# Average pooling over one axis: sixteen tile loads dealt out to two DMA queues

## The chip, the core and the metric

The kernel runs on one core of one Trainium2 chip. The time is device microseconds (us) from the start to the end of one execution; a median of several runs is quoted, and a profile comes from one execution of its own. Five engines of the core can issue instructions: TensorE (PE, not used here), VectorE (DVE), ScalarE (ACT), GpSimd (POOL) and SyncE (SP). Transfers between the chip's memory (HBM) and the on-chip buffers (SBUF) are done by 16 DMA engines. An instruction on SP's or on ACT's queue starts a transfer; it then runs by itself and raises a semaphore when it has landed.

## The reference

The input is 32 x 256 rows of 4096 float32 values. Each row is cut into 256 windows of 16 values, and the output is the mean of each window.

```python
batch, channels, length = 32, 256, 4096
output_size = 256
result = np.zeros((batch, channels, output_size), dtype=np.float32)
for i in range(output_size):
    start = int(i * length / output_size)
    end = int((i + 1) * length / output_size)
    result[:, :, i] = np.mean(x[:, :, start:end], axis=-1)
```

134.22 MB are read, 8.39 MB are written, and each input value takes part in one addition.

## The kernel before

The 8192 rows are put on 128 partitions and cut into 16 tiles. A tile has four rows in each partition (`R = 4`), which are 16,384 float32 values or 64 KB in one piece; a whole tile is 8.39 MB. It has 1024 windows (`cells`) in each partition, and `m = 512` is half of them.

The loop runs over `t` from 0 to 15. For each tile:

- **Load (L64).** One DMA on SP's queue fills the buffer `xin`. The pool `inpool` has two buffers, so tile t+2 goes into the buffer of tile t: its load waits until the last instruction that reads tile t is done. SP's queue holds all the loads, in order, and the loads of tiles 0 and 1 wait for nothing.
- **POOL (L68)** adds, in the second half of the windows, the upper eight values onto the lower eight, in place.
- **DVE (L73)** sums the first half of the windows, 16 values each. It needs nothing from POOL.
- **DVE (L76)** sums the second half of the windows, of which eight values each are left. It needs POOL's result, and it is the last reader of `xin`.
- **ACT (L79)** multiplies the tile's 1024 sums by 1/16, in place in the result tile. It reads no `xin`.

Results stay on the chip until the end: tile 0's in `res_first` and the others' in `res_rest`. In the last turn of the loop three stores are issued on SP's queue: tile 0's result (L66, 512 KB) and the results of tiles 1 to 14 (L67, 7168 KB), both after the last load in the queue, and tile 15's result (L85, 512 KB) at the end.

The program is written with a tile framework that puts in the semaphore waits. It also settles where each instruction stands in the queue of its engine; an engine takes the instructions of its queue in that order. In SP's queue before, they stand as in the source: 16 loads, then the three stores.

Of the kernel before, what the change touches and what calls it, by code (L numbers as in the profile page):

```python
# [1 line left out]

# [4 lines left out]


@with_exitstack
def kernel(  # L10
    ctx: ExitStack,
    tc: tile.TileContext,
    x: bass.AP,
    output_size: int,
    out: bass.AP,
):

    nc = tc.nc
    F32 = mybir.dt.float32
    X = mybir.AxisListType.X

    batch, channels, length = x.shape
    ob, oc, olen = out.shape
    assert ob == batch and oc == channels and olen == output_size
    assert length % output_size == 0
    window = length // output_size  # L30
    hw = window // 2
    inv_w = 1.0 / float(window)

    P = nc.NUM_PARTITIONS
    R = 4
    rows = batch * channels
    assert rows % (P * R) == 0
    ntiles = rows // (P * R)
    many = (ntiles - 1) * R
    cells = R * output_size  # L40
    m = cells // 2
    cols = R * length

    xr = x.rearrange("b c l -> (b c) l")
    orow = out.rearrange("b c o -> (b c) o")
    x_first = xr[0 : P * R, :].rearrange("(p r) l -> p (r l)", p=P, r=R)
    o_first = orow[0 : P * R, :].rearrange("(p r) o -> p (r o)", p=P, r=R)
    x_rest = xr[P * R :, :].rearrange("(p r) l -> p (r l)", p=P, r=many)
    o_rest = orow[P * R :, :].rearrange("(p r) o -> p (r o)", p=P, r=many)

    inpool = ctx.enter_context(tc.tile_pool(name="inpool", bufs=2))
    respool = ctx.enter_context(tc.tile_pool(name="respool", bufs=1))
    res_first = respool.tile([P, cells], F32, name="res_first")
    res_rest = respool.tile([P, (ntiles - 1) * cells], F32, name="res_rest")
    held = (ntiles - 2) * cells

    for t in range(ntiles):
        xin = inpool.tile([P, cells, window], F32, name="xin")
        if t == 0:
            res, base, src = res_first, 0, x_first  # L60
        else:
            res, base = res_rest, (t - 1) * cells
            src = x_rest[:, (t - 1) * cols : t * cols]
        nc.sync.dma_start(out=xin.rearrange("p o w -> p (o w)"), in_=src)  # L64
        if t == ntiles - 1:
            nc.sync.dma_start(out=o_first, in_=res_first[:, :])  # L66
            nc.sync.dma_start(out=o_rest[:, 0:held], in_=res_rest[:, 0:held])  # L67
        nc.gpsimd.tensor_add(  # L68
            out=xin[:, m:cells, 0:hw],
            in0=xin[:, m:cells, 0:hw],  # L70
            in1=xin[:, m:cells, hw:window],
        )
        nc.vector.reduce_sum(  # L73
            out=res[:, base : base + m], in_=xin[:, 0:m, :], axis=X
        )
        nc.vector.reduce_sum(  # L76
            out=res[:, base + m : base + cells], in_=xin[:, m:cells, 0:hw], axis=X
        )
        nc.scalar.mul(  # L79
            out=res[:, base : base + cells],  # L80
            in_=res[:, base : base + cells],
            mul=inv_w,
        )
        if t == ntiles - 1:
            nc.sync.dma_start(out=o_rest[:, base:], in_=res[:, base:])  # L85


# [1 line left out]
_INS = ['x', 'output_size']  # L89
_OUTS = [((32, 256, 256), 'float32')]  # L90

_NUMBERS = {'output_size': 256}


# [26 lines left out]
```

## Time and profile before

| What | Time |
|---|---|
| Median of 3 runs | 335.19 us (335.05 to 335.36) |
| The profiled execution, its own time | 334.91 us |
| Its span, first to last instruction in the trace | 333.1 us |
| DVE busy | 209.7 us (63%), 32 reductions |
| POOL busy | 139.7 us (42%), 16 additions |
| ACT busy | 18.2 us (5%), 16 multiplications |
| Transfers | 142.61 MB, 428 GB/s over the span |

The share of an engine is its busy time over the span. A row of the page that starts with a line number (L68) names a group of like instructions, how many there were, the mean duration of one in ns, and the time in which the engine stood idle before them, with what ended it. In the timeline the columns are the start in us, the duration in us, the engine, and the instruction; "SPq" is the queue of SP, and a row there is the issue of a transfer and not the transfer itself.

### The profile page before, as it was taken

The numbers are of one execution on the slowest core, as the hardware profiler recorded it, in microseconds if no ns is written. First come the engines' busy times: TensorE is split into PE (matmuls) and PEld (weight loads), VectorE is DVE, ScalarE is ACT, GpSimd is POOL, SyncE is SP. The second block draws the span as 40 slices with busy tenths as digits, with TensorE's granted clock in tenths as the row PEclk, the third lists the DMA queues.
The fourth block names the chain that finished last, engine by engine and source line by source line (L and its number), as shares of the span: only waits on it lengthen the run. The fifth ranks groups of instructions, "written<-read, shape, count | busy, mean of one in ns | idle before, by whom it ended". The sixth has DMA issues, their size and how long they took to land.

```text
span 333.1 us, 159 instructions
## 1 busy us (share of the span) xinstructions
DVE 209.7 (63%) x32; ACT 18.2 (5%) x17; POOL 139.7 (42%) x20
## 2 busy tenths in 40 slices
DVE  0029396693929569392957839295784929578491
ACT  1000101000010100001010100101010010101001
POOL 0027090643709063370906336090733609073460
DMA  9898989999898989999898989989898989989996
GB/s 378 378 504 378 504 378 464 417 393 488 378 504 378 504 378 472 409 401 480 378 504 378 504 378 464 417 386 496 378 504 378 504 378 464 417 386 496 409 441 283
DMA packets 2736, 142.61 MB, mean 428 GB/s; under 512 B 304, under 2 KB 304, under 8 KB 560
## 3 DMA queue, kind: packets, MB, share of 16 engines
q1 hardware_dynamic: 2736, 142.61, 99.1%
HBM read 134.22 MB, written 8.39 MB: 428 GB/s over the span
## 4 chain that ended last, share of the span: by engine, by line
DMA 66%; POOL 18%; DVE 11%; POOLq 3%; issue 0%; ACT 0%; SPq 0%
DMA xin<-in_x_dram 66%; POOL xin L68 18%; DVE res_rest L76 11%; POOLq L116 3%; ACT res_rest L79 0%; SPq L64 0%; POOLq L68 0%
## 5 line engine op out<-in xcount | busy, mean ns | idle before, releaser
L68 POOL TENSOR_TENSOR xin<-xin 128x4096 f32<-128x4096 f32 x16 | 139.5, 8717 | 181.8 <-DMA xin<-in_x_dram 181.8
L73 DVE TENSOR_REDUCE res_rest<-xin 128x512 f32<-128x8192 f32 x15 | 130.3, 8686 | 91.2 <-DMA xin<-in_x_dram 91.2
L76 DVE TENSOR_REDUCE res_rest<-xin 128x512 f32<-128x4096 f32 x15 | 66.3, 4420 | 2.6 <-POOL xin L68 2.4
L79 ACT ACTIVATE res_rest<-res_rest 128x1024 f32<-128x1024 f32 x15 | 15.8, 1056 | 274.5 <-DVE res_rest L76 274.5
L73 DVE TENSOR_REDUCE res_first<-xin 128x512 f32<-128x8192 f32 x1 | 8.7, 8686 | 22.6 <-DMA xin<-in_x_dram 22.6
L76 DVE TENSOR_REDUCE res_first<-xin 128x512 f32<-128x4096 f32 x1 | 4.4, 4419 | 0.1
L79 ACT ACTIVATE res_first<-res_first 128x1024 f32<-128x1024 f32 x1 | 1.1, 1056 | 33.8 <-DVE res_first L76 33.8
L79 ACT ACT_TABLE_LOAD x1 | 1.3, 1283 | 0.7 <-PEq L102 0.7
L102 POOL MEMSET const-float32-0.0<- 128x1 f32 x1 | 0.1, 98 | 0.2 <-issue 0.2
L102 POOL MEMSET const-bfloat16-1.0<- 128x1 bf16 x1 | 0.1, 101 | 0.0
L102 POOL MEMSET const-uint8-127<- 128x1 uint8 x1 | 0.1, 101 | 0.0
L102 POOL MEMSET const-float32-1.0<- 128x1 f32 x1 | 0.1, 98 | 0.0
## 6 DMA issues: line engine op xcount, KB each, us to landing
out_dram<-res_rest SPq DMA_DIRECT2D x1, 7168.0 KB, 23.1
out_dram<-res_first SPq DMA_DIRECT2D x1, 512.0 KB, 26.2
out_dram<-res_rest SPq DMA_DIRECT2D x1, 512.0 KB, 4.9
xin<-in_x_dram SPq DMA_DIRECT2D x16, 25.4
```

Source lines behind the costliest of these rows:

```text
L68: nc.gpsimd.tensor_add(out=xin[:, m:cells, 0:hw], in0=xin[:, m:cells, 0:hw], in1=xin[:, m:cells, hw:window],)
L73: nc.vector.reduce_sum(out=res[:, base : base + m], in_=xin[:, 0:m, :], axis=X)
L76: nc.vector.reduce_sum(out=res[:, base + m : base + cells], in_=xin[:, m:cells, 0:hw], axis=X)
L79: nc.scalar.mul(out=res[:, base : base + cells], in_=res[:, base : base + cells], mul=inv_w,)
L102: nc = _bacc.Bacc("TRN2", target_bir_lowering=False, num_devices=1)
L116: with _tile.TileContext(nc) as tc:
```

## The change

The loads of tiles 1, 3, 5 and so on stay on SP's queue; those of tiles 2, 4, 6 and so on go to ACT's queue. The load of tile 0 is cut by columns into two transfers of 32 KB for each partition, one on each queue. Of the stores, tile 0's and tile 15's go to ACT's queue; the large one stays on SP's.

```diff
-        nc.sync.dma_start(out=xin.rearrange("p o w -> p (o w)"), in_=src)
+        xin_2d = xin.rearrange("p o w -> p (o w)")
+        if t == 0:
+            half = cols // 2
+            nc.sync.dma_start(out=xin_2d[:, 0:half], in_=src[:, 0:half])
+            nc.scalar.dma_start(out=xin_2d[:, half:], in_=src[:, half:])
+        else:
+            queue = nc.sync if t % 2 else nc.scalar
+            queue.dma_start(out=xin_2d, in_=src)
         if t == ntiles - 1:
-            nc.sync.dma_start(out=o_first, in_=res_first[:, :])
+            nc.scalar.dma_start(out=o_first, in_=res_first[:, :])
             nc.sync.dma_start(out=o_rest[:, 0:held], in_=res_rest[:, 0:held])
...
         if t == ntiles - 1:
-            nc.sync.dma_start(out=o_rest[:, base:], in_=res[:, base:])
+            nc.scalar.dma_start(out=o_rest[:, base:], in_=res[:, base:])
```

In the built program, ACT's queue then stands as follows (`mul` is the multiplication of a tile):

```
load 0 (second half), table load, mul 0, load 2, mul 1, store of tile 0, mul 2,
load 4, mul 3, mul 4, load 6, mul 5, mul 6, load 8, ... load 14,
mul 13, mul 14, mul 15, store of tile 15
```

SP's queue holds the first half of load 0, the loads 1, 3, 5 to 15, and the large store. On ACT the load of tile t+2 carries no wait on DVE of its own, since it stands behind `mul t`, which waits for L76 of tile t.

## The prediction

> **What bounds the kernel now.** I read the transfers first, then the chain that ended last, then one period in the timeline, then the tail. The transfers, from the page (row by slice in tenths, packets, queue with its share of the 16 engines' span):
>
> ```profile
> DMA  9898989999898989999898989989898989989996
> DMA packets 2736, 142.61 MB, mean 428 GB/s; under 512 B 304, under 2 KB 304, under 8 KB 560
> q1 hardware_dynamic: 2736, 142.61, 99.1%
> ```
>
> The DMA engines work 99.1% of the span, so no wait on a compute engine costs time yet. Packets: 2736 less 560 small ones is 2176, which is 16 loads x 128 partitions = 2048 of 64 KB and 128 of the large store. A load is thus 8 packets on each of 16 engines.
>
> The chain that ended last, in order of time, its start and one period of it (start, duration, what):
>
> ```profile
> 0.73 0.37 SPq L64
> 1.10 0.05 issue
> 1.15 40.74 DMA xin<-in_x_dram
> ...
> 274.16 0.09 issue
> 274.25 8.73 POOL xin L68
> 282.98 0.02 issue
> 283.01 4.43 DVE res_rest L76
> 287.44 0.02 issue
> 287.45 25.37 DMA xin<-in_x_dram
> ```
>
> This looks as if compute were on the path. The timeline of the same stretch, and of the end, says why it is not:
>
> ```profile
> 22.60 8.69 DVE L73 TENSOR_REDUCE res_first<-xin 128x512 f32<-128x8192 f32 x1 [22.60 <-DMA xin<-in_x_dram]
> ...
> 274.14 8.69 DVE L73 TENSOR_REDUCE res_rest<-xin 128x512 f32<-128x8192 f32 x1 [6.08 <-DMA xin<-in_x_dram]
> 287.45 0.33 SPq L64 DMA_DIRECT2D xin<-in_x_dram  x1
> 287.46 1.06 ACT L79 ACTIVATE res_rest<-res_rest 128x1024 f32<-128x1024 f32 x1 [18.30 <-DVE res_rest L76]
> 293.49 8.69 DVE L73 TENSOR_REDUCE res_rest<-xin 128x512 f32<-128x8192 f32 x1 [6.06 <-DMA xin<-in_x_dram]
> 307.88 0.34 SPq L67 DMA_DIRECT2D out_dram<-res_rest  x1
> 312.84 8.69 DVE L73 TENSOR_REDUCE res_rest<-xin 128x512 f32<-128x8192 f32 x1 [6.08 <-DMA xin<-in_x_dram]
> 327.24 0.33 SPq L85 DMA_DIRECT2D out_dram<-res_rest  x1
> ```
>
> Tile 13 lands at 274.14, tile 14 at 293.49, tile 15 at 312.84: a load takes L = 19.35 us (433 GB/s; 2.42 us a packet). From tile 13's landing to the issue of load 15 it is 13.31 us. So load 15 is issued while load 14 still has 293.49 - 287.45 = 6.04 us to go, and queues behind it. These 6.04 us are all the slack that two buffers leave. The span is: tile 0 lands at 22.60, 15 x 19.35 = 290.24 to 312.84, then 8.39 MB of stores, of which the last is issued at 327.24 and lands 4.9 later (the page's DMA issues), 1.0 to the end: 333.1. With 1.8 around it the profiled run is 334.91; the median is 0.28 above.
>
> **The change, part by part.**
>
> *Nothing to win on volume.* The same 142.61 MB pass the same engines. Idle are at most 0.9% of 333.1 = 3.0 us, nearly all at start and end. The halved first load brings the two halves at one time: 8.39 MB either way, 0 us; 128 more packets and one more issue (0.33 us) lie under the wait for the data. ACT's table load (1.28 us) moves behind that issue and has until 35.85: 0.
>
> *Ten issues on ACT.* Seven whole loads, a half and two stores: 10 x 0.33 to 0.42 = 3.3 to 4.2 us on an engine that stands idle 274.5 us before its multiplications: 0 in busy time. Behind a waiting load on ACT stands `mul t+1`, which is due 19 us later and whose result only a store wants: 0. If that cover went, each would cost its 0.3 us.
>
> *A later issue.* Before, SP issued 0.02 us after L76. Now the even loads stand behind `mul t`: x = 1.06 us if the queue holds the issue until the multiplication is over, 0.02 if it does not, 1.39 if the issue takes its 0.33 after it as well. No row shows it. I take 1.06. By itself it lies inside the 6.04.
>
> *Tile 0's store* moves from behind load 15 to the time of load 3: 512 KB at 433 GB/s = 1.2 us, less at the end, more in the middle: 0. Tile 15's store follows its multiplication either way (327.24), and the large store, which ends later, hides it: 0. The large store still waits for `mul 14`, behind load 15 in SP's queue.
>
> *Two loads in flight on two queues: the step that decides.* Before, load t+2 could only follow load t+1. Now it stands in another queue, and nothing in the program makes it wait. No row of before has two queues, so the bounds are: the older load is served first (lands as now, price 0), or both get half, and a load with r us left lands r late. How much is left? A transfer takes some time from issue to its first byte: at least 0.42 us (the chain has the first DMA from 1.15, issue 0.73), at most 21.87 - 19.35 = 2.52 (first load, 0.73 to 22.60). So of the 6.04 the two overlap for S = 3.5 to 5.6; I take the middle, 4.6, since the first load's 2.52 also holds the start from an empty memory.
>
> With halves: load t+1 lands r late, so its compute and the issue of load t+3 are r late, while load t+2 has got r ahead. The next overlap is S - r, and less x if the next is issued on ACT. From ACT load to ACT load the overlap thus falls by x: the j-th sees S - jx. With 4.6 and 1.06 these are 3.5, 2.5, 1.4, 0.4, then -0.7, -1.8, -2.8, and the eighth in this chain, the large store behind `mul 14`, -3.9. A negative number is a time in which both queues are empty: nothing is left to move until the multiplication of the late tile is over. The sum is 0.7 + 1.8 + 2.8 + 3.9 = 9.2 us, and 335.19 + 9.2 = 344.4. Bounds: S = 5.6 gives 0.8 + 1.8 + 2.9 = 5.5 (340.7); S = 3.5 gives 14.3 (349.5); x = 0.02 gives no drift and 0 us; x = 1.39 with S = 4.6 gives 18.7 (353.9).
>
> If the queues take turns by whole packets instead, the overlap is rounded: 4.6 us is two packets left and a delay of 2.42, which leaves 4.6 - 2.42 - 1.06 = 1.1 us for the next ACT load: no gap, 0 us. But with three packets left (over 4.84 us, which the 1.2 us of tile 0's store beside load 3 can bring about) the delay is 4.84, and each ACT load from tile 6 on, and the large store, meets a gap of 4.84 + 1.06 - 4.6 = 1.3 us: 6 x 1.3 = 7.8 (343.0).
>
> The row for sharing is the 99.1% above: full engines have no rate to give a second queue. [...]
>
> **The rivals.**
>
> *Older load first (or turns that stay balanced): no change.* Place: the 6.04 us before each landing. It decides if the load ahead is delayed by no more than S - x = 3.5 us at each ACT load. For it: before shows strict order in one queue, and the balanced case above. Against: nothing orders two queues. Time: 335.2, with 0.1 to 0.3 either way for packets and start: 334.9 to 335.6.
>
> *Faster: store beside load.* Tile 0's store reads the buffers that loads write; on two queues the two directions might pass at once. That saves at most its 1.2 us, and perhaps a few tenths of the first load's 2.5 us start: 335.19 - 1.2 = 334.0. Against: the stores of before run at the loads' pace (8.39 MB between 312.84 and 332.1, 436 GB/s), so an engine is the limit either way.
>
> *Much slower: convoy.* If a load ahead is delayed until both land together, the queues stay empty for two tiles' compute, 2 x 13.3 less their overlap, in each pair: tens of us, over 353. For it: x of 1.39 or an S of 3.5 brings the gaps to 5 to 8 us by the end. Against: the built order has load t+2 ahead of `mul t+1`, so ACT never holds it for the other tile.
>
> **How the numbers follow.** Sharing with gaps 0.54 (344.4; its own range 340.5 to 351), older first or balanced 0.33 (335.2), store beside load 0.08 (334.0), convoy 0.05. A difference under 0.2% (0.67 us) is no change here, which is about what runs of this kernel can tell. So faster 0.08, same 0.33, slower 0.59. The range takes in the no-change case and the sharing case up to 351: 334.9 to 351.
>
> **What would show it.** In the profile after: two queues, 2880 packets (128 for the halves, 16 for one more transfer). Right: landings (starts of the first DVE reduction) at uneven distances, one near 14 to 15 us and the next near 24 to 26, zeros or low digits in the DMA row that grow towards the end, even loads issued 1.1 us after their L83. Wrong: landings 19.35 us apart throughout, or alternating about 17 and 22 with the DMA share still at 99%; an even load issued beside its multiplication (x near 0); the odd loads' time to landing not above the 25.4 of before.

## The result, and the profile after

The kernel after takes 343.56 us (median of 5 runs, 343.26 to 344.0) beside 335.05 us before (5 runs, 334.99 to 335.36): a ratio of 1.0253, 95% interval 1.0241 to 1.0264. It is 2.5% slower. The profiled span grew from 333.1 to 342.2 us, by 9.1.

The page of the kernel after, the same rows as before:

```profile
DMA  8999998998989899999899999998999998999796
DMA packets 2880, 142.61 MB, mean 417 GB/s; under 512 B 320, under 2 KB 320, under 8 KB 576
q1 hardware_dynamic: 1440, 78.64, 53.4%
q10 hardware_dynamic: 1440, 63.96, 44.2%
```

SP's queue is q1, ACT's is q10. Together they fill 97.6% of 342.2 us, which is 334.0; before it was 99.1% of 333.1, which is 330.1. The bytes are the same. So of the 9.1 us, 5.2 are time in which DMA engines had nothing to do (8.2 against 3.0), and 3.9 are packets that took longer.

The chain of waits of the kernel after, in order of time, one period (start, duration, what):

```profile
161.06 8.73 POOL xin L75
169.79 0.02 issue
169.81 4.43 DVE res_rest L83
174.24 0.02 issue
174.26 26.71 DMA xin<-in_x_dram
```

The links are those of before; the compute took no longer (8.73 and 4.43). The transfer's link was 25.37 and is 26.71. The timeline of the kernel after, around two of ACT's loads (start, duration, engine; SPq and ACTq are issues):

```profile
117.57 0.33 ACTq L71 DMA_DIRECT2D xin<-in_x_dram  x1
121.13 8.69 DVE L80 TENSOR_REDUCE res_rest<-xin 128x512 f32<-128x8192 f32 x1 [3.65 <-DMA xin<-in_x_dram]
...
134.44 0.33 SPq L71 DMA_DIRECT2D xin<-in_x_dram  x1
...
146.44 8.69 DVE L80 TENSOR_REDUCE res_rest<-xin 128x512 f32<-128x8192 f32 x1 [12.03 <-DMA xin<-in_x_dram]
...
159.75 1.06 ACT L86 ACTIVATE res_rest<-res_rest 128x1024 f32<-128x1024 f32 x1 [24.26 <-DVE res_rest L83]
159.84 0.33 ACTq L71 DMA_DIRECT2D xin<-in_x_dram  x1
160.95 8.69 DVE L80 TENSOR_REDUCE res_rest<-xin 128x512 f32<-128x8192 f32 x1 [1.23 <-DMA xin<-in_x_dram]
...
186.50 8.69 DVE L80 TENSOR_REDUCE res_rest<-xin 128x512 f32<-128x8192 f32 x1 [12.27 <-DMA xin<-in_x_dram]
...
200.99 8.69 DVE L80 TENSOR_REDUCE res_rest<-xin 128x512 f32<-128x8192 f32 x1 [1.21 <-DMA xin<-in_x_dram]
```

Landings are read from the starts of a tile's first reduction. Tiles 5 to 9 land at 121.13, 146.44, 160.95, 186.50 and 200.99: distances of 25.3, 14.51, 25.55 and 14.49 where it was 19.35 each time. Load 8 is issued at 159.84, when the load ahead of it has 1.1 us to its landing and not 6.04; its first packet comes 1.32 us after the issue, too late to follow on. The trace's records of single DMA packets show the hole (times in us of the span, shifted as in the last section): all 16 DMA engines have a packet under way up to 159.0, 6 of them at 160.0, none at 161.0, and all 16 again at 161.75. Between 157 and 165 an engine stands idle for 1.4 us on average; before, in the same stretch, for none.

The DMA row of the page does not show it: its digits are 8 and 9 nearly throughout, as before. It counts a packet where it starts, and so do windows of a few us: with packets of 2.42 us, a window of 4 us of the kernel before (201 to 205) reads 0.68 although its engines are full.

The engines are full until the hole, and it comes once for each pair of tiles. A pair took 2 x 19.35 = 38.70 us. From landing 5 to 7, 7 to 9 and so on to 15 the five pairs take 39.82, 40.04, 40.37, 40.25 and 40.10: 7.1 us more in all. Another 1.8 are there by landing 5, of which 1.2 is tile 0's store (512 KB at the loads' 433 GB/s, an estimate), moved from the end to this place. That is 8.9 of the 9.1. A sixth hole stands behind landing 15: the large store is issued at 321.60, 0.11 before that landing, where it was issued 4.96 before. From landing 15 to the end it is 20.5 us, where it was 20.3 with 512 KB more to store.

### The profile page after: what moved, and what is told of

The parts are those of the page before. It is cut to its first block, busy times and chain, and to the rows that moved or that the text cites. A ratio compares the mean times of both kernels' runs of the same rounds, so it can differ in the third digit from the quotient of the medians.

```text
span 342.2 us, 163 instructions
## 1 busy us (share of the span) xinstructions
DVE 209.7 (61%) x32; ACT 18.2 (5%) x17; POOL 139.7 (41%) x20
## 2 busy tenths in 40 slices
DMA packets 2880, 142.61 MB, mean 417 GB/s; under 512 B 320, under 2 KB 320, under 8 KB 576
## 4 chain that ended last, share of the span: by engine, by line
DMA 66%; POOL 18%; DVE 10%; POOLq 3%; issue 0%; ACT 0%; SPq 0%
DMA xin<-in_x_dram 66%; POOL xin L75 18%; DVE res_rest L83 10%; POOLq L123 3%; ACT res_rest L86 0%; SPq L67 0%; POOLq L75 0%
## 6 DMA issues: line engine op xcount, KB each, us to landing
out_dram<-res_first ACTq DMA_DIRECT2D x1, 512.0 KB, 24.8
```

## The experiments

All ratios are against the kernel before, run beside it on the same chip.

**Both queues in use, but no load can overtake.** Each tile's load is cut in two, as only tile 0's was:

```diff
-        if t == 0:
-            half = cols // 2
-            nc.sync.dma_start(out=xin_2d[:, 0:half], in_=src[:, 0:half])
-            nc.scalar.dma_start(out=xin_2d[:, half:], in_=src[:, half:])
-        else:
-            queue = nc.sync if t % 2 else nc.scalar
-            queue.dma_start(out=xin_2d, in_=src)
+        half = cols // 2
+        nc.sync.dma_start(out=xin_2d[:, 0:half], in_=src[:, 0:half])
+        nc.scalar.dma_start(out=xin_2d[:, half:], in_=src[:, half:])
```

> Every tile's load is cut into two halves, one on SP's and one on ACT's queue, so both queues are in use all the time but no load can overtake the one ahead of it in either. Theory of turns (the younger load takes packets' turns from the older one): nothing is delayed, 335.0 to 335.8 us, landings 19.35 us apart, DMA share 99%. Rival (ACT's queue, or two queues as such, are slower): 343 us or more, since twice as many loads touch ACT's queue.

336.56 us, ratio 1.0047 (1.0032 to 1.0062). The page of this run has the two queues filled almost evenly, 99.2% together:

```profile
DMA packets 5040, 142.61 MB, mean 426 GB/s; under 512 B 560, under 2 KB 560, under 8 KB 816
q1 hardware_dynamic: 2448, 74.45, 51.9%
q10 hardware_dynamic: 2592, 68.16, 47.3%
```

Landings are 19.40 to 19.44 us apart throughout. It is 0.8 us above the expected range. The 15 landing distances are 0.08 us longer each, 1.2 in all. There are twice as many packets of half the size, and in the packet records one takes 1.218 us (median), so two take 2.436 where one of 64 KB took 2.420. Two queues at work the whole time leave no holes.

**All loads on ACT's queue.**

```diff
-            queue = nc.sync if t % 2 else nc.scalar
-            queue.dma_start(out=xin_2d, in_=src)
+            nc.scalar.dma_start(out=xin_2d, in_=src)
```

(The branch for tile 0 goes as well.)

> All loads on ACT's queue, the stores as in the kernel after. Theory of turns: one queue, the older load is served first; 335.0 to 335.5 us. Rival (loads issued from ACT come late, behind the multiplication, or run slower): with 14 loads instead of 7 behind a multiplication, 343 us or more.

335.40 us, ratio 1.0011 (1.0002 to 1.002). ACT's queue carries loads as well as SP's: with 14 loads behind a multiplication there are 0.4 us, not 8.5. One distance is not 19.35: the last is 21.52, and that is the one load beside which a transfer on the other queue was issued, the large store.

**Tile 0's store, two tries.** Moved to SP's queue in the source:

```diff
-            nc.scalar.dma_start(out=o_first, in_=res_first[:, :])
+            nc.sync.dma_start(out=o_first, in_=res_first[:, :])
```

> As the kernel after, but tile 0's store goes back to SP's queue, behind the last load. If the store of 512 KB in the middle of loads 3 and 4 is what tips the balance of turns: landings alternate 17 and 22 us apart to the end, 335.0 to 336 us. If the turns alone do it: gaps come all the same, 340 to 345 us.

343.67 us, ratio 1.0259 (1.0231 to 1.0286). This run tells nothing of the store's place: its issue stands at 37.36 us in the timeline, between loads 1 and 3, because the framework put it there. So the store was tied to late data (`zero` is a new tile of one column, and the issue further up is taken out):

```diff
+        if t == ntiles - 2:
+            nc.scalar.mul(out=zero[:, :], in_=res[:, base : base + 1], mul=0.0)
+            nc.gpsimd.tensor_add(
+                out=res_first[:, 0:1], in0=res_first[:, 0:1], in1=zero[:, :]
+            )
+            nc.scalar.dma_start(out=o_first, in_=res_first[:, :])
```

> As the kernel after, but tile 0's store is held back to the end: POOL adds to one column of it a zero that ACT makes from tile 14's result, so that it stands behind the last load again. If the store in the middle is what tips the balance of turns: landings 17 and 22 us apart to the end, 335.0 to 336 us. If two queues alone do it: the same gaps, landings 14.5 and 25.5 us apart in the later half, 340 to 345 us.

344.89 us, ratio 1.0292 (1.0275 to 1.0309). The store is issued at 315.12, and the landings are 24.8 to 25.7 and 14.5 apart from tile 5 to tile 14 all the same (the last distance is 22.28). Here it is SP's loads (tiles 5, 7 and so on) that land late and not ACT's. So the store in the middle is not needed for the holes, and which queue suffers is no property of the queue.

**Tile 0's load whole.**

```diff
-        if t == 0:
-            half = cols // 2
-            nc.sync.dma_start(out=xin_2d[:, 0:half], in_=src[:, 0:half])
-            nc.scalar.dma_start(out=xin_2d[:, half:], in_=src[:, half:])
-        else:
-            queue = nc.sync if t % 2 else nc.scalar
-            queue.dma_start(out=xin_2d, in_=src)
+        queue = nc.sync if t % 2 or t == 0 else nc.scalar
+        queue.dma_start(out=xin_2d, in_=src)
```

> As the kernel after, but tile 0's load is whole and on SP's queue, so loads 0 and 1 follow each other as before, and only loads 2, 4 to 14 and the two stores are on ACT's queue. Theory of turns: the halved first load is not needed for it; 340 to 346 us, landings that end up some 14.5 and 25.5 us apart. Rival (the halved first load, which delays tile 0, sets off the unevenness): 335 to 336 us.

344.23 us, ratio 1.0272 (1.0249 to 1.0295), landings 25.2 to 25.8 and 14.5 apart from tile 6 on. The halves are not needed for it.

**The alternation alone undone.**

```diff
-            queue = nc.sync if t % 2 else nc.scalar
-            queue.dma_start(out=xin_2d, in_=src)
+            nc.sync.dma_start(out=xin_2d, in_=src)
```

> The kernel after with the alternation alone undone: load 0 is halved over both queues and the two small stores stay on ACT's, but loads 1 to 15 are all on SP's queue. Theory of turns: no load can be overtaken, landings 19.35 us apart, 335.0 to 335.8 us. If the halves or the stores have a part in the loss: 337 us or more.

335.24 us, ratio 1.0008 (0.9998 to 1.0017). With the halves and the moved stores kept, the whole loss is gone, and from tile 3 on the landings are 19.34 to 19.37 apart. So it takes the alternation to make the loss.

**A later issue, on two queues and on one.** After the multiplication, a small ACT instruction writes 32 columns of the buffer that is to be loaded next, so that the issue waits for it (with `t % 2 == 0` on two queues, without on one):

```diff
+        if t % 2 == 0 and t < ntiles - 2:
+            nc.scalar.mul(out=xin_2d[:, 0:32], in_=res[:, base : base + 32], mul=1.0)
```

> As the kernel after, but before each load on ACT's queue a small ACT instruction writes the result of the multiplication into the buffer that is about to be loaded, so that the issue has to wait for the end of the multiplication: it comes about 1.3 us later than in the kernel after. Theory of turns with empty queues: each such load adds its delay to a gap that is there, 5 to 7 times 1.3 us, 350 to 353 us. Rival (the loss is transfer rate, which two queues share badly, and not waiting): the delay lies inside the 6 us of slack and the time stays at 343 to 344.5 us.

355.24 us, ratio 1.0604 (1.0586 to 1.0622). The timeline of this run:

```profile
110.74 8.69 DVE L80 TENSOR_REDUCE res_rest<-xin 128x512 f32<-128x8192 f32 x1 [13.84 <-DMA xin<-in_x_dram]
...
125.17 0.23 ACT L92 ACTIVATE xin<-res_rest 128x32 f32<-128x32 f32 x1
125.24 8.69 DVE L80 TENSOR_REDUCE res_rest<-xin 128x512 f32<-128x8192 f32 x1 [1.19 <-DMA xin<-in_x_dram]
125.49 0.33 ACTq L71 DMA_DIRECT2D xin<-in_x_dram  x1
...
152.18 8.69 DVE L80 TENSOR_REDUCE res_rest<-xin 128x512 f32<-128x8192 f32 x1 [13.66 <-DMA xin<-in_x_dram]
...
166.70 8.69 DVE L80 TENSOR_REDUCE res_rest<-xin 128x512 f32<-128x8192 f32 x1 [1.21 <-DMA xin<-in_x_dram]
```

The load is issued 0.25 us after the landing of the load ahead, when nothing at all is under way. A pair takes 41.46 us (125.24 to 166.70), 1.4 more than in the kernel after, and the holes begin at tile 2. The total is 2 us above the expected range, and far from what lost rate alone would give.

On one queue:

> All loads on ACT's queue, and before each of them the same small ACT instruction as in the run with the dose, so that every issue comes about 1.3 us late, 14 of them. Theory of turns: the older load is served first and 4.6 us of real slack swallow 1.3, 335.2 to 335.8 us. If the late issue costs time by itself: 14 x 1.3 = 18 us, 353 us.

337.04 us, ratio 1.0063 (1.0048 to 1.0078), 1.2 above the expected range. The timeline of this run:

```profile
78.59 0.33 ACTq L65 DMA_DIRECT2D xin<-in_x_dram  x1
83.17 8.69 DVE L74 TENSOR_REDUCE res_rest<-xin 128x512 f32<-128x8192 f32 x1 [6.02 <-DMA xin<-in_x_dram]
...
102.52 8.69 DVE L74 TENSOR_REDUCE res_rest<-xin 128x512 f32<-128x8192 f32 x1 [6.04 <-DMA xin<-in_x_dram]
```

From tile 2 to tile 14 the landings are 19.35 apart, although each load is issued 1.4 us later (78.59, when the reduction ended at 77.16). So the delay itself is swallowed, and 18 us are not there. The extra time comes at both ends: load 2 now stands behind tile 0's store, the distances to landings 1 and 2 are 0.75 and 1.66 longer; the last landing comes 21.49 after the one ahead, beside the large store as in the run with all loads on ACT's queue, and the last store is issued at 331.95, when the large one has all but landed (310.46 and 21.8 to landing). Landing 1 is late because the last packet of load 1 on every engine, begun between 39.1 and 39.7, takes 3.0 to 3.3 us in the packet records instead of 2.42; what slows it is not known.

**Four buffers of half the size,** first on two queues, then on one:

```diff
-    R = 4
+    R = 2
...
-    inpool = ctx.enter_context(tc.tile_pool(name="inpool", bufs=2))
+    inpool = ctx.enter_context(tc.tile_pool(name="inpool", bufs=4))
```

> The kernel after with tiles of half the size (two rows per partition) and four buffers, so the same memory holds three loads ahead of the one in use. Theory of turns: a load that is overtaken is late, but two more are queued, so the queues do not run empty; DMA share 99%, within 1.5 us of the same tiles on one queue, 335 to 337 us. Rival (two queues in use cost rate as such): 343 us or more.

> The kernel before with the same smaller tiles and four buffers, all on SP's queue, as the measure for the run with two queues. Both theories: 335 to 336.5 us, since the DMA engines were full already and twice as many half-size packets cost about 1 us.

Two queues: 342.16 us, ratio 1.0215 (1.0199 to 1.023). One queue: 337.19 us, ratio 1.0066 (1.0051 to 1.0081). One queue is 0.7 above its expected range, for two queues the expectation was missed by 5 us, which brings the time next to the rival's (343 or more). The windows (stretch in us, its length, busy time and count of DVE, ACT and POOL, clock, DMA share, GB/s) tell where the 5 us are; first two queues, then one:

```profile
280.00:305.00 25.00, 13.22 (x4) 1.55 (x3) 8.87 (x2) 1.00 1.01 432
305.00:320.00 15.00, 14.73 (x5) 1.26 (x2) 13.32 (x3) 1.00 0.57 244
```

```profile
280.00:305.00 25.00, 15.99 (x6) 1.89 (x3) 9.34 (x3) 1.00 1.02 440
305.00:320.00 15.00, 11.81 (x4) 0.63 (x1) 8.90 (x2) 1.00 0.99 427
```

With more loads queued there are no holes on the way (DMA share 1.01 and 1.02 up to 305, and no idle time from 30 to 305 in the packet records of either), as the theory has it, and no rate is lost by the two queues as such: both kernels have moved 130.2 MB by 305. But two tiles now land together, and at the end, where no further load is queued, the engines wait for the compute of both: share 0.57 for 15 us. The large store is issued at 319.18 instead of 312.59. The expectation had left out the end.

**More slack.** The second half of the windows is left out on both sides, first on two queues, then on one:

```diff
-        nc.gpsimd.tensor_add(
-            out=xin[:, m:cells, 0:hw],
...
-        nc.vector.reduce_sum(
-            out=res[:, base + m : base + cells], in_=xin[:, m:cells, 0:hw], axis=X
-        )
+    nc.vector.memset(res_first[:, :], 0.0)
+    nc.gpsimd.memset(res_rest[:, :], 0.0)
```

> As the kernel after, but the second half of the windows is left out (POOL's addition and the second reduction; zeros are written there), so that a buffer is free 8.7 us after landing instead of 13.3, and a load is issued with 10.6 us of the one ahead to go instead of 6.0. Theory of turns: the delay of the load ahead grows with what is left of it, about 9.2 us rounded up to whole packets and one turn for the semaphore, 9.7 to 12 us; that leaves 9.7 to 7.3 us of the next against 8.7 + 1.5 until its successor starts, so there are gaps of 0.5 to 3 us for each pair again, 339 to 355 us. Rival (the slack of 6 us was a little too thin, more of it would hide the sharing): 334 to 336 us.

> The kernel before with the same part of the computation left out, all on SP's queue, as the measure for the run with two queues. Both theories: the transfers set the time, 334 to 335.5 us.

Two queues: 345.52 us, ratio 1.0313 (1.0293 to 1.0333). One queue: 335.07 us, ratio 1.0002 (0.9992 to 1.0011). The timeline of the run on two queues:

```profile
152.54 8.69 DVE L77 TENSOR_REDUCE res_rest<-xin 128x512 f32<-128x8192 f32 x1 [21.78 <-DMA xin<-in_x_dram]
...
161.33 0.34 ACTq L73 DMA_DIRECT2D xin<-in_x_dram  x1
162.25 8.69 DVE L77 TENSOR_REDUCE res_rest<-xin 128x512 f32<-128x8192 f32 x1 [1.01 <-DMA xin<-in_x_dram]
...
192.84 8.69 DVE L77 TENSOR_REDUCE res_rest<-xin 128x512 f32<-128x8192 f32 x1 [21.91 <-DMA xin<-in_x_dram]
```

A third less compute makes the kernel on two queues no faster; the holes are as large as before (161.33 against a landing at 162.25). At both sizes that were run, 6.0 and 10.6 us, the slack is given away: a load issued earlier delays the one ahead by more.

## Why the prediction came out as it did

The forecast was 344.4 us by holes that sharing two queues makes; 343.56 was measured. The mechanism is shown by four pairs: holes with the alternation and none without it, none where both queues carry halves of the same tile, a dose of delay that adds on two queues and is swallowed on one, and slack that does not help. The terms inside were not all right, and some made up for others: that the number is off by only 0.8 us is luck.

*What bounds the kernel, and volume.* As predicted: 99.1% before, 2880 packets after, compute durations unchanged, and no gain from the halves (ratio 1.0008 with halves and stores kept). The second queue brought no rate: 417 GB/s over the span where it was 428, and 2.5% more time.

*The later issue, x = 1.06 us: wrong.* ACT's queue does not hold the issue for the multiplication. In the timeline after, the multiplication starts at 159.75 and the issue at 159.84, 0.09 later, and 13.40 after landing 6 where it was 13.31. An even load issued beside its multiplication was one of the prediction's own signs of being wrong. The drift from pair to pair by 1.06, on which the sum of 9.2 rested, does not exist: the five pairs lose 1.1 to 1.7 each, with no growth after the third, and holes that grow towards the end, one of the signs of being right, are not there. With x near 0.02, the sum of 9.2 becomes 0. (The other estimate in it was good: I took 1.47 us from issue to first byte, the middle of two bounds, and load 8's first packet comes 1.32 after its issue.)

*Equal halves: wrong; turns by whole packets: right.* Where loads 8 and 9 overlap, from 176 to 187 us, the packet records hold in order of time 16 packets of load 8, 16 of load 9, 16 of load 8, 16 of load 9 (one for each DMA engine), and then the 16 packets of 4 bytes that end load 8. The distances between landings are 19.35 less whole packets of 2.42 us: 16.93 is one (104.20 to 121.13, early in the kernel after), 14.51 is two, 9.67 is four (the run with less compute). So the side estimate by packets, 343.0, described the machine, and the headline number came from the other one. It held 1.3 us for a pair; measured are 1.36 in a typical one (40.06, from landing 6 to landing 8). In the packet records of one such period (161.16 to 201.22) an engine is idle for 0.63 us on average and its packets take 0.73 longer, 1.36 together. But its parts were other: 0.09 instead of 1.06 for x, and in place of the rest a term I did not have. A load that started into empty engines had slow first packets: in the packet records, the first 16 packets of load 8 take 3.12 us on average instead of 2.42 (the first 16 of load 0 in the kernel before took 3.10), and the 16 engines start up to 0.34 apart. So load 8 needs 22.9 us from its first packet to its last, which is 19.35, one packet of the other queue (2.42) and 1.1 more. The loop from landing 6 to landing 8 is 13.40 to the issue, 1.32 to the first packet, 22.9, and 2.4 for the semaphore (below): 40.0. With x at 0.09, the prediction's sum by packets gives 6 x 0.33 = 2 us; only the 1.1 us for each of the six holes, 6.6 in all, which it put at nothing, bring it to 343.8 (an estimate from these figures).

*The size of a turn.* If a load's eight pieces and its 4-byte packet on one engine had gone in one turn, the older load would have been served whole, and the time would have stayed at the 335.2 of the rival that has the older load first (an estimate from the time before). The packet records show a smaller turn: from 176 to 187 us the queue changes after every 64 KB piece, 2.42 us.

*What tips the balance.* I had named tile 0's store as what may lead to a third packet of delay. It is not needed (344.89 us with the store at the end). What makes the step from distances of 17 and 22 to 14.5 and 25.5 near tile 6 is open: load 6 is issued 3.6 us before landing 5, and its first packet comes 0.9 before it on some DMA engines and 0.5 after it on the last. The idle time there is small (0.08 us on average over the engines between 116 and 124), but the first 16 packets of load 6 take 2.92 us on average. So a first loss at this place is likely, but no run tried it alone.

*The rivals.* Older load first is refuted as a whole (landings 14.5 and 25.5 us apart where it has 19.35), though it holds on the way in (below). A store beside a load saved nothing (ratio 1.0008 with tile 0's store beside load 2). The convoy did not come with two buffers; tiles that land together did, with four, and cost their 5 us at the end.

## What to carry to other kernels

In this kernel, whose DMA engines were full, a second queue brought no rate (ratio 1.0047 with halves of every tile on both), but it took away an order that the first one gave for nothing: the oldest load, whose landing leads to the next buffer coming free, is no longer served first (landings 14.5 and 25.5 us apart instead of 19.35). More slack did not protect against it (345.52 us with 10.6 us of slack), since the load that is issued early delays the one ahead by more; an order did, by one queue (335.40) or by halves of the same tile on both (336.56). To see it in a profile, look at the distances between landings and at how long before the landing ahead a load is issued, not at the mean DMA share of 97.6%.

## What was not expected

The delay of a load is in good part the delay of its semaphore. The trace's packet records have for each load the data packets of 64 KB and, on each of the 16 engines, a last packet of 4 bytes. The landing follows the last of these by 0.02 to 0.11 us in the table, so they are taken here for what raises the semaphore. In us of the span, for the kernel after (the packets' times are shifted by one constant, 0.35 us, which makes the 4-byte packets meet the landings; whether this is a difference of clocks or a time that the semaphore needs is not shown, so a first packet may have come 0.35 earlier after its issue than the columns say):

```
load  queue  issue   first packet  last data end  last 4-byte packet  landing
1     SP       1.16      22.04          42.06           44.47           44.57
2     ACT     36.32      41.37          61.38           61.38           61.49
6     ACT    117.57     120.18         144.01          146.42          146.44
7     SP     134.44     138.29         160.91          160.91          160.95
8     ACT    159.84     161.16         184.05          186.46          186.50
```

Before, the 4-byte packet follows the last data at once (load 14: 293.36 and 293.36, reduction at 293.49). After, load 1's data end at 42.06, near the landing of 41.92 before, but its semaphore stands in its queue's next turn, behind one 64 KB packet of load 2: 2.41 us. The same 2.4 us stand at the end of loads 6 and 8. So of the two packets by which ACT's loads are late, one is the other load's data and one is the wait of 4 bytes for their turn. And a load that was issued beside a busy queue began late: load 2's first packet comes 5.05 us after its issue, load 8's, with empty engines, 1.32.
